# Layer norms of a two-layer decoder trunk: rows g and b applied to x later and on VectorE, their loads spread, a third weight block split ahead, and the order around the norm pinned

## The chip, the cores and the metric

One Trainium2 chip, one core of it. The metric is the device time of one execution in microseconds (us). A core has five engines that run side by side, each in the order of its own queue: TensorE (PE; matmuls and transposes), VectorE (DVE), ScalarE (ACT), GpSimd (POOL) and SyncE (SP, which here only issues DMAs). POOL issues DMAs too, through a queue of its own. They wait for each other by semaphores.

## The reference

A decoder trunk of two layers over 256 positions of width 2048, all in float32. Layer 0 mixes by a gated DeltaNet (GDN), layer 1 by sparse attention (DSA). What the change touches is the norm behind the mixer and behind the FFN, and what stands around it:

```python
def layer_norm(x, g, b):
    mu = mean(x); var = mean((x - mu) ** 2)
    return (x - mu) * rsqrt(var + LN_EPS) * g + b

for i in range(2):
    h = gdn_mixer(x, ...) if i == 0 else dsa_mixer(x, ...)
    x = layer_norm(DN_ALPHA * x + h, ln1_g[i], ln1_b[i])
    f = (silu(causal_dwconv(x @ ffn_w_gate[i])) * (x @ ffn_w_up[i])) @ ffn_w_down[i]
    x = layer_norm(DN_ALPHA * x + f, ln2_g[i], ln2_b[i])
    x = x + sigmoid(x @ ple_w_gate[i]) * (p[i] @ ple_w_proj[i])
```

## The kernel before

x lies in SBUF as two halves of 128 positions (a = 0, 1) by 2048. Every product with a weight matrix runs through `weights` (L89): a block of 128x1024 numbers (512 KB) is loaded by SP (`raw`, pool wp), rounded by ACT to the format that TensorE takes (`hi`), and DVE computes the rest, `lo` = raw − hi (both pool hl). TensorE then sums three products, x_hi·hi, x_lo·hi and x_hi·lo. The pools set how far this runs ahead: raw has 4 buffers, hi and lo have 2 each, so while TensorE works on one block the next is split, and further ones are being loaded. The splits carry a high priority (`W_AHEAD`), so the scheduler puts them early on ACT and DVE; the order on each engine is fixed when the program is built.

The two forms of product: in `gemm_t_steps` (GDN input, FFN gate and up) weights are stationary and the transposed activations move: x_hi and x_lo stand side by side as 512 columns (L117), then x_hi alone with lo as 256 (L121). In `gemm_steps` (the projections back to x, the PLE) the activations are stationary and 512 or 256 columns of weights move (L141, L142, L145).

`project` (the mixer's output or w_down) goes over five column blocks of x; behind each, DVE adds the residual (L214) and takes its statistics (L215). Behind the last one TensorE has two small products of the PLE (`fill`, L678 copies them to pw), meant for the time in which the norm's statistics are made. Then `layer_norm` (L241): DVE makes mean and 1/sqrt (a chain of twelve small instructions, L248 to L252), DVE and ACT normalise one half of x each, four pieces of 512 columns (L256, L257), TensorE transposes (L261, `n_ps`), ACT applies g and b, which lie along the partitions there, (L266, `xb`), and DVE splits the result into `xT` (L268 rounds, a CAST; L269 subtracts), the operand of the next products. The next product can begin with the first of eight xT pieces.

x itself gets g and b too, since it is added to the next residual: as rows along the columns. Rows of 512 columns (lng, lnb; broadcast to 128 partitions, 256 KB, two buffers each) are loaded by POOL (L194), and POOL multiplies and adds them (L274, L275): 16 instructions per norm, right behind it.

After the norm of the mixer comes the FFN: 20 pairs of column blocks, each gate and up (four weight blocks each), with the activation of gate ended by a Silu on ACT (L635). After the norm of the FFN comes the PLE: four column blocks of w_gate with 8 weight blocks each, the first two of them in turn. In layer 0's FFN, `distances` also writes the bias table `fx` for DSA to DRAM: four broadcasts of 766 KB (L724), issued by POOL as soon as fd is there.

GDN runs in eight groups. In each, SP carries a matrix L through DRAM and back (`lt` L464, `ld` L467), POOL makes inverses from it (L480, L482), which go back through `tt` and `pm` to TensorE (`w_ps`, L492). SP issues lt and ld in one queue with the loads of raw.

Of the kernel before, what the change touches and what calls it, by code (L numbers as in the profile page):

```python
# [63 lines left out]
class Trunk:  # L64
    def __init__(self, nc, tc, ctx, t):
# [21 lines left out]
        self.xT = self.xtp.tile([P, KT, 2, S], F32R, tag="xT", name="xT")  # L87


    def weights(self, src, rows, nk, cols):  # L90
# [8 lines left out]
        with self.tc.high_priority(offset=W_AHEAD):  # L99
            nc.scalar.activation(hi, raw, AF.Copy)  # L100
            nc.vector.tensor_tensor(lo, raw, hi.bitcast(F32), op=ALU.subtract)  # L101
# [27 lines left out]
    def gemm_steps(self, src, c0, n, x, kt, done):  # L129
# [5 lines left out]
        for k0 in range(0, kt, nk):  # L135
# [7 lines left out]
            for k in range(m):  # L143
                for a in range(2):
                    nc.tensor.matmul(ps[a][:, :n], x(k0 + k)[:, 0, a * P:(a + 1) * P], lo[:, k, :], start=False,  # L145
                                     stop=k0 + k == kt - 1)
# [44 lines left out]
    def rows(self, pool, src, n, tag, bufs=1):  # L191

        r = pool.tile([P, n], F32, tag=tag, name=tag, bufs=bufs)
        self.nc.gpsimd.dma_start(out=r, in_=bass.AP(tensor=src.tensor, offset=src.offset, ap=[[0, P], [1, n]]))  # L194
        return r
# [45 lines left out]
    def layer_norm(self, pool, st, g, b, gb):  # L241

        nc, x, xT = self.nc, self.x, self.xT
        with self.tc.high_priority():
# [7 lines left out]
            nc.vector.scalar_tensor_tensor(nm, mv[:, 1, 0:1], -1.0, r[:, 1:2], op0=ALU.mult, op1=ALU.mult)  # L252
            for k0 in range(0, KT, 2):
                if k0 % 4 == 0:
                    x0, x1 = (x[:, a, k0 * P:(k0 + 4) * P] for a in range(2))
                    nc.vector.tensor_scalar(x0, x0, mv[:, 0, 0:1], r[:, 0:1], op0=ALU.subtract, op1=ALU.mult)  # L256
                    nc.scalar.activation(x1, x1, AF.Identity, scale=r[:, 1:2], bias=nm)  # L257
                ps = self.sp.tile([P, 2, S], F32, tag="bk" if k0 % 4 else "sp", name="n_ps")
                for k in range(2):
                    for a in range(2):  # L260
                        nc.tensor.transpose(ps[:, k, a * P:(a + 1) * P], x[:, a, (k0 + k) * P:(k0 + k + 1) * P],  # L261
                                            self.ident)
                xb = pool.tile([P, 2, S], F32, tag="xb", name="xb", bufs=2)
                for k in range(2):
                    gk, bk = gb[:, k0 + k:k0 + k + 1], gb[:, KT + k0 + k:KT + k0 + k + 1]
                    nc.scalar.activation(xb[:, k], ps[:, k], AF.Identity, scale=gk, bias=bk)  # L266
# [3 lines left out]
        for nb in range(4):  # L270
            cs = slice(nb * 512, (nb + 1) * 512)
            gr, br = (self.rows(pool, r[cs], 512, k, 2) for r, k in ((g, "lng"), (b, "lnb")))
            for a in range(2):
                nc.gpsimd.tensor_tensor(x[:, a, cs], x[:, a, cs], gr, op=ALU.mult)  # L274
# [610 lines left out]
```

## Time and profile before

| | us |
|---|---|
| three runs | 2957.22, 2959.93, 2960.61 |
| median | 2959.93 |
| the profiled execution: its own time | 2958.56 |
| its span | 2956.8 |
| granted clock of TensorE, mean | 0.988 |
| loads of raw, 512 KB, issue to landing (median, most weights) | 3.6 |
| lng, lnb, 256 KB | 5.9, 6.2 |
| fx, 766 KB | 11.1 |
| POOL L274, one instruction (least, median, most) | 1.26, 1.51, 2.29 |
| DVE L268 CAST (least, median, most) | 0.41, 1.49, 1.52 |

The span goes from the first to the last instruction. A row of the timeline gives the start, the duration, the engine, the line and the operation, the tile written and those read, and in brackets how long the engine had been idle and what ended that. A row of windows gives, for a stretch from A to B, its length and the busy time of PE, of its weight loads, of DVE, ACT and POOL (with the number of instructions), then the granted clock, the busy share of the DMA engines and GB/s. A row of waits gives engine, tile and line, what it waited for, the sum, the number of times and the longest.

### The profile page before, as it was taken

To read this page: it belongs to the slowest core of one execution; us is meant where nothing else is said; L and a number is where in the kernel's file an instruction comes from. 1 tells how busy PE (TensorE), PEld (TensorE's weight loads), DVE (VectorE), ACT (ScalarE), POOL (GpSimd) and SP (SyncE) were. 2 spreads that over 40 slices of the span, in tenths; PEclk is the share of its full clock that TensorE was granted. 3 is DMA by queue.
4 is the path that set the end of the run, shared out by engine and by line. 5 is a ranking of instruction groups with operands and counts; after the bars stand their busy time and mean duration, and the time that the engine had idled before them with its cause. 6 is when DMAs were issued, how large, how long until landed. Compare 5 with 4: busy or idle time off the path is not lost. (4 is left out here: it accounts for less than half of the span.)

```text
span 2956.8 us, 41860 instructions
## 1 busy us (share of the span) xinstructions
PE 2842.5 (96%) x15790; PEld 2450.5 (83%) x15790; DVE 1904.7 (64%) x3080; ACT 1398.1 (47%) x2143; POOL 490.0 (17%) x780
## 2 busy tenths in 40 slices
PE   8899999999899899999999899999989999999989
PEld 6688888888679788888888788888878888888877
DVE  6678777788454856666554755656586666655475
ACT  4445455455333545555433444455355555543344
POOL 1543344543300300000000300120040000000030
PEclk9899999999999999999999999999999999999999
DMA  7555556655465566666555456554656666655545
GB/s 195 148 143 147 156 159 166 163 147 145 137 221 187 162 213 186 189 188 189 190 192 191 149 184 197 171 164 136 221 161 186 192 186 191 187 192 192 192 148 180
DMA packets 425883, 520.94 MB, mean 176 GB/s; under 512 B 28204, under 2 KB 329648, under 8 KB 425424
## 3 DMA queue, kind: packets, MB, share of 16 engines
q1 hardware_dynamic: 418576, 499.91, 55.8%
q0 software_dynamic: 7104, 18.35, 2.2%
q8 instruction: 124, 2.03, 0.3%
q14 instruction: 79, 0.65, 0.1%
HBM read 513.94 MB, written 7.39 MB: 176 GB/s over the span
## 5 line engine op out<-in xcount | busy, mean ns | idle before, releaser
L101 DVE TENSOR_TENSOR lo<-raw,hi 128x1024 fp32r<-128x1024 f32 x925 | 1161.5, 1257 | 883.5 <-ACT hi L100 863.3
L100 ACT ACTIVATE hi<-raw 128x1024 fp32r<-128x1024 f32 x925 | 977.3, 1057 | 1305.4 <-PE b_ps L142 563.8
L117 PE MATMUL mm_ps<-xT,hi 128*128 128x512 f32 x4176 | 1075.4, 397 | 13.2 <-ACT hi L100 7.9
L117 PEld LDWEIGHTS mm_ps<-xT,hi 128*128 128x128 f32 x4176 | 751.6, 190 | 149.0 <-ACT hi L100 9.0
L121 PEld LDWEIGHTS mm_ps<-xT,lo 128*128 128x128 f32 x4176 | 571.1, 190 | 46.9 <-DVE lo L101 7.8
L121 PE MATMUL mm_ps<-xT,lo 128*128 128x256 f32 x4176 | 594.8, 284 | 6.1 <-DVE lo L101 6.1
L274 POOL TENSOR_TENSOR x<-x,lng 128x512 f32<-128x512 f32 x32 | 51.4, 1626 | 1507.8 <-PE n_ps L261 1421.7
L141 PE MATMUL b_ps<-hi,xT 128*128 128x512 f32 (+2 forms) x736 | 276.1, 381 | 5.7 <-ACT hi L100 5.7
L142 PE MATMUL b_ps<-hi,xT 128*128 128x512 f32 (+2 forms) x736 | 276.5, 381 | 0.8 <-DVE xT L269 0.8
L141 PE MATMUL b_ps<-hi,hTA 128*128 128x512 f32 (+1 forms) x640 | 212.5, 347 | 0.0
L142 PE MATMUL b_ps<-hi,hTA 128*128 128x512 f32 (+1 forms) x640 | 212.3, 347 | 0.0
L145 PE MATMUL b_ps<-lo,xT 128*128 128x512 f32 (+2 forms) x736 | 196.5, 384 | 5.2 <-DVE lo L101 5.2
L141 PEld LDWEIGHTS b_ps<-hi,xT 128*128 128x128 f32 x736 | 139.6, 190 | 30.8 <-ACT hi L100 6.5
L142 PEld LDWEIGHTS b_ps<-hi,xT 128*128 128x128 f32 x736 | 140.0, 190 | 25.7 <-DVE xT L269 1.6
L145 PEld LDWEIGHTS b_ps<-lo,xT 128*128 128x128 f32 x736 | 133.0, 191 | 30.7 <-DVE lo L101 6.9
L145 PE MATMUL b_ps<-lo,hTA 128*128 128x512 f32 (+1 forms) x640 | 138.6, 347 | 0.0
L141 PEld LDWEIGHTS b_ps<-hi,hTA 128*128 128x128 f32 x640 | 121.2, 189 | 15.0
L142 PEld LDWEIGHTS b_ps<-hi,hTA 128*128 128x128 f32 x640 | 121.2, 189 | 15.0
L480 POOL TENSOR_TENSOR xt<-ld,xi 128x60 f32<-128x60 f32 (+24 forms) x248 | 116.7, 471 | 96.2 <-DMA ld<-lt 77.4
L145 PEld LDWEIGHTS b_ps<-lo,hTA 128*128 128x128 f32 x640 | 105.1, 189 | 15.0
L141 PE MATMUL b_ps<-hi,oT 128*128 128x512 f32 (+1 forms) x320 | 107.1, 350 | 3.4 <-ACT hi L100 3.4
L482 POOL TENSOR_TENSOR xi<-xi,xt 128x60 f32<-128x60 f32 (+24 forms) x248 | 106.9, 431 | 19.4
(260 smaller groups left out, 2727.2 us busy)
## 6 DMA issues: line engine op xcount, KB each, us to landing
raw<-in_gdn_w_in SPq DMA_DIRECT2D x193, 512.0 KB, 3.9
raw<-in_ffn_w_gate SPq DMA_DIRECT2D x160, 512.0 KB, 3.6
raw<-in_ffn_w_up SPq DMA_DIRECT2D x160, 512.0 KB, 3.6
raw<-in_ffn_w_down SPq DMA_DIRECT2D x160, 512.0 KB, 3.6
raw<-in_dsa_w_in SPq DMA_DIRECT2D x80, 512.0 KB, 3.6
raw<-in_gdn_w_o SPq DMA_DIRECT2D x64, 512.0 KB, 3.7
raw<-in_ple_w_gate SPq DMA_DIRECT2D x64, 512.0 KB, 4.2
raw<-in_dsa_w_o SPq DMA_DIRECT2D x32, 512.0 KB, 3.6
```

The lines of the kernel that those rows point to most:

```text
L100: nc.scalar.activation(hi, raw, AF.Copy)
L101: nc.vector.tensor_tensor(lo, raw, hi.bitcast(F32), op=ALU.subtract)
L117: nc.tensor.matmul(q[:m, :], hi[:, k, o:o + m], x[:, k0 + k].rearrange("p a b -> p (a b)"), start=k0 + k == 0, stop=False)
L121: nc.tensor.matmul(q[:m, S:], lo[:, k, o:o + m], x[:, k0 + k, 0, :], start=False, stop=k0 + k == kt - 1)
L141: nc.tensor.matmul(ps[a][:, :n], xh, hi[:, k, :], start=k0 + k == 0, stop=False)
L142: nc.tensor.matmul(ps[a][:, :n], xl, hi[:, k, :], start=False, stop=False)
L145: nc.tensor.matmul(ps[a][:, :n], x(k0 + k)[:, 0, a * P:(a + 1) * P], lo[:, k, :], start=False, stop=k0 + k == kt - 1)
L274: nc.gpsimd.tensor_tensor(x[:, a, cs], x[:, a, cs], gr, op=ALU.mult)
L480: nc.gpsimd.tensor_tensor(tmp[:, :m, :w], bcast(ld[:, i + 1:, i], m, 1), xi[:, :m, i:i + 1].to_broadcast([P, m, w]), op=ALU.mult)
L482: nc.gpsimd.tensor_tensor(xi[:, :m, i + 1:], xi[:, :m, i + 1:], tmp[:, :m, :w], op=ALU.subtract)
```

## The change

- hi and lo get three buffers each instead of two, raw three instead of four. To make room, GDN's `sq` shares a buffer with `y0`, and `ot` with `y` (two buffers).
- `layer_norm` takes over the order by explicit dependences: the splits of the next two blocks stand behind DVE's first piece of x (`behind`), the last copies of pw behind ACT's first piece, ACT's later pieces behind its xb, all transposes behind the last matmul of the fillers (`self.last`). The first piece of x is halved, to 256 columns.
- g and b on x: the 64 instructions move from POOL to DVE, out of the norm. For LN1 they are placed in the FFN, a quarter each after the steps n = 6, 14, 22, 30; the row loads wait for that step's last Silu (`self.mark`). For LN2 they are placed in the PLE behind the first three weight blocks of its first two column blocks, all four quarters, with no such wait. lng and lnb have one buffer each.
- fx is written in eight pieces of 383 KB, each behind the Silu of a step.

```diff
-        self.hl = pool(name="hl", bufs=2)
+        self.hl = pool(name="hl", bufs=3)
-        self.wp = pool(name="wp", bufs=4, side="right")
+        self.wp = pool(name="wp", bufs=3, side="right")
...
+    def after(self, ins, to, sync=False):
+        kind = mybir.DependencyClass.Sync if sync else mybir.DependencyClass.NoSync
+        self.tc.add_manual_dep(ins.ins, to.ins.name, mybir.DependencyInfo(kind, mybir.DependencyReason.DATA),
+                               reason="order")
...
-            nc.vector.tensor_tensor(lo, raw, hi.bitcast(F32), op=ALU.subtract)
+            ins = nc.vector.tensor_tensor(lo, raw, hi.bitcast(F32), op=ALU.subtract)
+        if self.behind:
+            self.after(ins, self.behind.pop())
...
-                if k0 % 4 == 0:
-                    x0, x1 = (x[:, a, k0 * P:(k0 + 4) * P] for a in range(2))
+                n = 2 if k0 < 4 else 0 if k0 % 4 else 4
+                if n:
+                    x0, x1 = (x[:, a, k0 * P:(k0 + n) * P] for a in range(2))
...
+                    if k0 >= 4:
+                        self.after(act, parts[k0 // 4 - 1])
+                    if not k0:
+                        self.behind = [dve] * 2
+                        for c in copies:
+                            self.after(c, act)
...
-        for nb in range(4):
-            gr, br = (self.rows(pool, r[cs], 512, k, 2) for r, k in ((g, "lng"), (b, "lnb")))
-            for a in range(2):
-                nc.gpsimd.tensor_tensor(x[:, a, cs], x[:, a, cs], gr, op=ALU.mult)
-                nc.gpsimd.tensor_tensor(x[:, a, cs], x[:, a, cs], br, op=ALU.add)
+        def affine(pool, nb, start):
+            gr, br = (self.rows(pool, r[cs], 512, k, 1, start) for r, k in ((g, "lng"), (b, "lnb")))
+            for a in range(2):
+                nc.vector.tensor_tensor(x[:, a, cs], x[:, a, cs], gr, op=ALU.mult)
+                nc.vector.tensor_tensor(x[:, a, cs], x[:, a, cs], br, op=ALU.add)
...
-                sq = pool.tile([P, 2, S], F32, tag="sq", name="sq")
+                sq = pool.tile([P, 2, S], F32, tag="y0", name="sq")
...
-                ot = pool.tile([P, 4, P], F32, tag="ot", name="ot")
+                ot = pool.tile([P, 4, P], F32, tag="y", name="ot", bufs=2)
...
+                if n in (6, 14, 22, 30):
+                    affine(pool, n // 8, self.mark)
...
+            for _ in range(3):
+                for g in steps[:2]:
+                    next(g)
+            for nb in range(4):
+                affine(pool, nb, None)
...
-        for o in range(0, R, R // 4):
+        for o in range(0, R, R // 8):
             yield
+            self.after(ins, self.mark, sync=True)
```

In the changed kernel's lines weights are L103 (raw), L107 (hi), L108 (lo); x is normalised on L270 and L271, transposed on L281, xb is L287, xT L290 and L291; rows of g and b are loaded on L203 and applied on L297 and L298.

The order on DVE at the first LN1, from the end of the statistics to the first xT pieces. Before:

```order
L238 SCALAR_TENSOR_TENSOR rs2_9302<-rt2_9303,rs2_9302 128x2
L101 TENSOR_TENSOR lo_9480<-raw_9477,hi_9479 128x1024
L252 SCALAR_TENSOR_TENSOR lnm_9316<-lmv_9297,rs2_9302 128x1
L256 TENSOR_SCALAR x_7845<-x_7845,lmv_9297,rs2_9302 128x512 x4
L268 CAST xT_84<-xb_9325 128x2x256
L269 TENSOR_TENSOR xT_84<-xb_9325,xT_84 128x2x256
```

After, at the same place:

```order
L249 SCALAR_TENSOR_TENSOR rs2_9302<-rt2_9303,rs2_9302 128x2
L264 SCALAR_TENSOR_TENSOR lnm_9316<-lmv_9297,rs2_9302 128x1
L270 TENSOR_SCALAR x_7845<-x_7845,lmv_9297,rs2_9302 128x256 x2
L270 TENSOR_SCALAR x_7845<-x_7845,lmv_9297,rs2_9302 128x512 x3
L108 TENSOR_TENSOR lo_9426<-raw_9423,hi_9425 128x1024
L108 TENSOR_TENSOR lo_9450<-raw_9447,hi_9449 128x1024
L290 CAST xT_84<-xb_9325 128x2x256
L108 TENSOR_TENSOR lo_9472<-raw_9469,hi_9471 128x1024
L291 TENSOR_TENSOR xT_84<-xb_9325,xT_84 128x2x256
```

Before, lo_9480 stands in the chain, and farther up, not shown, lo_9456 in the midst of the twelve small instructions and lo_9280 between the residual's statistics. After, the splits of the first FFN blocks stand between x and xT, three of them instead of two, and lo_9280 one residual earlier.

The order on DVE in the PLE of layer 0, from the end of the xT pieces on; lng and lnb are the rows of g and b. Before:

```order
L269 TENSOR_TENSOR xT_84<-xb_15532,xT_84 128x2x256
L101 TENSOR_TENSOR lo_15654<-raw_15651,hi_15653 128x1024
L101 TENSOR_TENSOR lo_15672<-raw_15669,hi_15671 128x1024
L101 TENSOR_TENSOR lo_15690<-raw_15687,hi_15689 128x1024
L101 TENSOR_TENSOR lo_15708<-raw_15705,hi_15707 128x1024
```

After:

```order
L298 TENSOR_TENSOR x_7845<-x_7845,lnb_15665 128x512
L108 TENSOR_TENSOR lo_15698<-raw_15695,hi_15697 128x1024
L297 TENSOR_TENSOR x_7845<-x_7845,lng_15671 128x512 x2
L108 TENSOR_TENSOR lo_15716<-raw_15713,hi_15715 128x1024
L298 TENSOR_TENSOR x_7845<-x_7845,lnb_15673 128x512 x2
L108 TENSOR_TENSOR lo_15734<-raw_15731,hi_15733 128x1024
L297 TENSOR_TENSOR x_7845<-x_7845,lng_15679 128x512 x2
L298 TENSOR_TENSOR x_7845<-x_7845,lnb_15681 128x512
L108 TENSOR_TENSOR lo_15752<-raw_15749,hi_15751 128x1024
L298 TENSOR_TENSOR x_7845<-x_7845,lnb_15681 128x512
```

Where splits followed each other, operations with rows stand between them now, and three more of these stand farther up between the xT pieces.

The order on SP in GDN, at group 7. Before:

```order
L96 DMA raw_7532<-in_gdn_w_in 128x2x512
L464 DMA lt_7055<-L_6974 32x8x32 x4
L96 DMA raw_7550<-in_gdn_w_in 128x2x512
L467 DMA ld_7060<-lt_7055 128x1x1024
L96 DMA raw_7568<-in_gdn_w_in 128x2x512
```

After:

```order
L103 DMA raw_7532<-in_gdn_w_in 128x2x512
L103 DMA raw_7550<-in_gdn_w_in 128x2x512
L489 DMA lt_7055<-L_6974 32x8x32 x4
L103 DMA raw_7568<-in_gdn_w_in 128x2x512
L492 DMA ld_7060<-lt_7055 128x1x1024
```

lt and ld each stand one load of raw later, in this group and in groups 1 to 6.

More of the change, by code (lines that the diff above doesn't have):

```diff
@@ L144, in gemm_steps @@
                 for a in range(2):
-                    nc.tensor.matmul(ps[a][:, :n], x(k0 + k)[:, 0, a * P:(a + 1) * P], lo[:, k, :], start=False,
-                                     stop=k0 + k == kt - 1)
+                    self.last = nc.tensor.matmul(ps[a][:, :n], x(k0 + k)[:, 0, a * P:(a + 1) * P], lo[:, k, :],
+                                                 start=False, stop=k0 + k == kt - 1)
             if k0 + m < kt:
@@ L189, in to_xT, with rows @@
         self.split(xT[:, k0:k0 + 4, 0, a * P:(a + 1) * P], xT[:, k0:k0 + 4, 1, a * P:(a + 1) * P], ps)
-    def rows(self, pool, src, n, tag, bufs=1):
+    def rows(self, pool, src, n, tag, bufs=1, start=None):
         r = pool.tile([P, n], F32, tag=tag, name=tag, bufs=bufs)
-        self.nc.gpsimd.dma_start(out=r, in_=bass.AP(tensor=src.tensor, offset=src.offset, ap=[[0, P], [1, n]]))
+        ins = self.nc.gpsimd.dma_start(out=r, in_=bass.AP(tensor=src.tensor, offset=src.offset, ap=[[0, P], [1, n]]))
+        if start is not None:
+            self.after(ins, start, sync=True)
         return r
@@ L239, in rsqrt, with layer_norm @@
         return y
-    def layer_norm(self, pool, st, g, b, gb):
+    def layer_norm(self, pool, st, g, b, gb, copies):
         nc, x, xT = self.nc, self.x, self.xT
@@ L260, in layer_norm @@
                     for a in range(2):
-                        nc.tensor.transpose(ps[:, k, a * P:(a + 1) * P], x[:, a, (k0 + k) * P:(k0 + k + 1) * P],
-                                            self.ident)
+                        ins = nc.tensor.transpose(ps[:, k, a * P:(a + 1) * P],
+                                                  x[:, a, (k0 + k) * P:(k0 + k + 1) * P], self.ident)
+                        self.after(ins, self.last)
                 xb = pool.tile([P, 2, S], F32, tag="xb", name="xb", bufs=2)
@@ L641, in up @@
                 self.split(hT(n)[:, 0], hT(n)[:, 1], h)
-            distances = self.distances(pool)
+            distances = self.distances(pool) if not i else iter(())
             for n in range(0, NF, 2):
```

49 lines of the change are left out of this document (27 added, 22 removed).

## The prediction

> **What bounds the kernel now.** I read the head of the page first, then the table of what TensorE waits for, then the windows around the waits.
>
> ```profile
> PE 2842.5 (96%) x15790; PEld 2450.5 (83%) x15790; DVE 1904.7 (64%) x3080; ACT 1398.1 (47%) x2143; POOL 490.0 (17%) x780
> ```
>
> TensorE (PE) is busy for 96% of the span, and no other engine is near that. So time is lost only where PE stands, and the change can gain no more than those places hold. The waits of PE, with the sum, the number and the longest of them:
>
> ```profile
> PE w_ps L492 <- DMA pm<-tt: 26.3, 2, 13.9
> ...
> PE b_ps L141 <- ACT hi L100: 9.0, 4, 2.8
> PE n_ps L261 <- DVE x L256: 8.8, 4, 2.2
> ...
> PE mm_ps L117 <- ACT hi L100: 7.9, 3, 3.5
> ...
> PE b_ps L145 <- DVE lo L101: 5.2, 4, 1.7
> ```
>
> Of these, those that come four times belong to the four layer norms. The windows show what they cost together: a quiet stretch first, then the first norm of a layer (LN1) and the second (LN2), both of layer 0.
>
> ```profile
> 900.00:950.00 50.00, 50.00 (x351) 47.04 (x350) 25.42 (x26) 19.06 (x18) 0.00 (x0) 1.00 0.60 188
> 963.00:1008.00 45.00, 35.56 (x190) 28.99 (x189) 42.87 (x54) 24.59 (x38) 29.39 (x20) 0.96 0.47 141
> 1661.00:1704.00 43.00, 33.56 (x143) 25.87 (x142) 40.21 (x49) 22.54 (x34) 28.75 (x20) 0.92 0.40 129
> ```
>
> In both, PE is idle for 9.4 us while VectorE (DVE, third busy time) is full: 42.87 of 45 us and 40.21 of 43. Inside a norm DVE is the bound. It is full for two reasons. The first is order, seen in its timeline (start, duration):
>
> ```profile
> 966.44 1.23 DVE L101 TENSOR_TENSOR lo<-raw,hi 128x1024 fp32r<-128x1024 f32 x1
> ...
> 969.45 1.23 DVE L101 TENSOR_TENSOR lo<-raw,hi 128x1024 fp32r<-128x1024 f32 x1
> ...
> 970.67 1.91 DVE L256 TENSOR_SCALAR x<-x,lmv,rs 128x512 f32<-128x512 f32 x4
> ```
>
> Splits of the blocks to come (lo) stand inside the chain of statistics, which ends where x is normalised (L256); a third one stands ahead of these two, as the rows of the order in the part on the change have it. The second reason is POOL:
>
> ```profile
> 972.51 2.67 POOL L274 TENSOR_TENSOR x<-x,lng 128x512 f32<-128x512 f32 x2 [152.93 <-PE n_ps L261]
> ...
> 984.51 0.58 POOL L194 DMA_DIRECT2D lng<-in_ln_g  x1
> ...
> 988.77 3.00 POOL L274 TENSOR_TENSOR x<-x,lng 128x512 f32<-128x512 f32 x2 [1.94 <-DMA lng<-in_ln_g]
> ```
> ```profile
> 975.65 1.51 DVE L268 CAST xT<-xb 128x512 fp32r<-128x512 f32 x1
> 977.20 1.64 DVE L269 TENSOR_TENSOR xT<-xb,xT 128x512 fp32r<-128x512 f32 x1
> ...
> 985.03 0.41 DVE L268 CAST xT<-xb 128x512 fp32r<-128x512 f32 x1
> 985.48 0.69 DVE L269 TENSOR_TENSOR xT<-xb,xT 128x512 fp32r<-128x512 f32 x1
> ```
>
> From 972.5 POOL multiplies and adds; beside it a piece of xT costs DVE 1.51 + 1.64 us. In POOL's pause (984.5 to 988.8, loads only) the same piece costs 0.41 + 0.69.
>
> **The change, term by term.** The profiled execution took 2958.56 us (span 2956.8 plus 1.8 around it), 1.4 under the median of the runs; the sum is made against 2958.56. Anything within 0.2% (some 6 us) a measurement of this kernel can't tell from no change.
>
> *LN1, twice.* PE's timeline of layer 0:
>
> ```profile
> 967.96 1.09 PE L145 MATMUL b_ps<-lo,pT 128*128 128x512 f32 x4
> 971.26 2.38 PE L261 MATMUL n_ps<-ident,x 128*128 128x128 f32 x17 [2.21 <-DVE x L256]
> ...
> 975.78 1.01 PE L117 MATMUL mm_ps<-xT,hi 128*128 128x512 f32 x3 [1.23 <-DVE xT L269]
> ...
> 1004.91 2.00 PE L117 MATMUL mm_ps<-xT,hi 128*128 128x512 f32 x8
> ...
> 1007.71 2.00 PE L117 MATMUL mm_ps<-xT,hi 128*128 128x512 f32 x8
> ```
>
> The last filler block ends near 969.1, the FFN's first matmul is at 975.78 and its ninth block at 1007.71; one undisturbed block is 2.8 (1007.71 − 1004.91). After: three lo's go out of the chain at 1.15 each (969.45 to just before 970.67), so x starts at 967.2. Its pieces on DVE (1.91 for four, now five with two of them halved) take some 2.2, two lo's 2.4, then CAST 0.41, lo 1.2, subtraction 0.69: the first matmul has its operand at 974.2, with handing over 974.5. PE has 24 transposes at 0.14 (2.38/17) ahead and 8 more behind (1.1), then eight blocks (22.4). Three are split already, and xT pieces come every 1.1 us instead of 3.15, so they run through (in the norm ACT's later x pieces, the pw copies and the transposes held behind the fillers only change places on engines that wait there anyway, so they cost nothing; if ACT lacked the time, rival 2 has the price): 974.5 + 1.1 + 22.4 = 998.0, with 0.4 for a late split 998.4. That is **−9.3 each, −18.6**. Bounds: −11.8 if nothing waits from 969.1 on (4.5 + 22.4 = 995.9), −3.4 if only the chain is shorter.
>
> *LN2, twice.*
>
> ```profile
> 1665.56 1.09 PE L145 MATMUL b_ps<-lo,pT 128*128 128x512 f32 x4
> ...
> 1702.86 1.07 PE L145 MATMUL b_ps<-lo,xT 128*128 128x512 f32 x4
> 1703.77 0.39 PE L141 MATMUL b_ps<-hi,xT 128*128 128x512 f32 x1
> ...
> 1705.58 1.07 PE L145 MATMUL b_ps<-lo,xT 128*128 128x512 f32 x4
> ```
>
> The fillers end at 1666.5 and the eighth PLE block starts at 1703.77; a block takes 2.72 (1705.58 − 1702.86). Without waits 32 transposes (4.5) and seven blocks (19.0) bring it to 1690.0. DVE needs the same run from lnm to the first xT piece, which costs PE about 0.9, and 0.9 for a late split: 1691.8, **−12.0 each, −24.0** (bounds −13.8 and −3.4).
>
> *Row operations on DVE.* The nearest row is
>
> ```profile
> L692 DVE TENSOR_TENSOR x<-x,sg x16: 678/686/694, 1728.6 to 2952.9; 128x512 f32<-128x512 f32 x16
> ```
>
> 64 of them at 0.69 are 44 us, spread over 16 quarters (2.7 each). In the FFN DVE is far from full (25.42 of 50 in the quiet window), so the work itself costs nothing. What can cost is the wait for the row: DVE works in order, so behind an x*g that waits for its load stand lo's for which PE waits. The load's time:
>
> ```profile
> DMA to landing us min/median/max: 3.5/5.9/9.5
> ```
> ```profile
> bias<-fx POOLq DMA_DIRECT2D x4, 256.0 KB, 4.7
> ```
>
> The 5.9 is for rows issued four at once; a row in its own comes nearer to 984.51 → 988.77 (4.3), and the 256 KB bias beside weight traffic took 4.7. I take 4.7. In the FFN the load leaves at the Silu, DVE does two lo's (one per 2.8 us), and comes to x*g 3 to 4 us later; it stands 1 to 2 us, while PE has blocks split for 4.5 us (POOL issues rows and fx pieces in turn, each behind the Silu of its own step, so none holds up the next): **0** (bounds 0 and +8, 1 us in each of eight). In PLE the order is tighter: row operations stand between the splits there, and each row has one buffer, so the load of lnb_15681 can leave only when DVE is done with lnb_15673. I followed it from 1661 with lo's of 1.2 and row operations of 0.69: the last use of lnb_15665 ends at some 1685.3; lnb_15673 lands at 1690.0 and its two operations end at 1691.4; lnb_15681 lands at 1696.1 and its operations, a lo between them, end at 1698.7; lnb_15689 lands at 1703.4, its operations end at 1704.8, and the lo behind them (the twelfth block's) at 1706.0. PE wants it at 1691.8 + 4 x 2.72 + 1.8 = 1704.5: **+1.5 each, +3**. With 4.3 a load it is 0.3, with 6.2 it is 6.0, since three loads stand in a row (bounds 0 and +12 for both layers). By the Trainium skill, DMA: Bandwidth & Descriptors, Anatomy of one DMA, a transfer of a POOL queue takes 2.0 us plus its bytes at 436 GB/s, an estimated 2.6 us for a row of 256 KB, and the term would be 0; the trace has nothing under 3.5, so I don't follow it.
>
> *fx.*
>
> ```profile
> 1071.94 1.11 PE L121 MATMUL mm_ps<-xT,lo 128*128 128x256 f32 x8
> 1076.54 3.78 PE L117 MATMUL mm_ps<-xT,hi 128*128 128x512 f32 x8 [3.48 <-ACT hi L100]
> ...
> 1083.94 1.11 PE L121 MATMUL mm_ps<-xT,lo 128*128 128x256 f32 x8
> ```
> ```profile
> fx<-fd POOLq DMA_DIRECT2D x4, 766.0 KB, 11.1
> ```
> ```profile
> 1076.50:1082.00 5.50, 5.46 (x17) 4.69 (x18) 2.45 (x2) 2.55 (x4) 0.00 (x0) 0.50 0.68 203
> ```
>
> Four pieces at once starve the weights. From one lo group to the one two blocks on are 12.0 us where two blocks are 5.6: 6.4 lost, 3.5 of them the wait and 2.9 the matmuls behind it, at a granted clock of 0.50. Pieces of half the size, one per two pairs of columns, should not do it: **−6.4** (other end 0).
>
> *Clock.* That row prices a pause of PE at up to its own length again. After the change each norm still has a pause of 1 to 2.5 us (PE waits for the first xT piece). Before, the transposes of LN2 behind a pause of 2.21 came at the lower clock, those of LN1 hardly. I add **+3** over four norms (bounds 0 and 4 × 2.9). The Trainium skill, TensorE: Matmul & The Clock Gate, Part 1, has half clock after an idle window of about 3.4 us that runs freely; by it the pauses left, all shorter, would mostly stay free and the term be near 0; the row behind 2.21 at LN2 (window's clock 0.92) speaks against that.
>
> *GDN.* Three blocks of raw weights instead of four, but three of hi/lo instead of two: six under way as before. Where the order of SP changes, lt and ld, which feed the inverses that w_ps waits for, each stand one raw later. In group 7 no other work covers that:
>
> ```profile
> 708.42 0.54 SPq L467 DMA_DIRECT2D ld<-lt  x1
> 712.25 0.39 SPq L96 DMA_DIRECT2D raw<-in_gdn_w_in  x1
> ```
>
> ld now stands behind raw_7568, which waits for a buffer and came at 712.25: ld at 712.6 instead of 708.42, and w_ps (the 26.3 above, of which this group is half) waits longer by as much. **+4** (bounds 0 and +4.2, as the splits may free the buffer sooner). In groups 1 to 6 other matmuls lie between; 0. The shared buffers of GDN (sq with y0, ot with y) make a square wait for the solve of the group before; the key blocks of the next group hide that, and without this cover eight groups would pay some 0.5 each: 0, bounds 0 and +4.
>
> Sum: −18.6 − 24.0 + 3 − 6.4 + 3 + 4 = −39.0; 2958.56 − 39.0 = **2919.6**.
>
> **Rivals.**
> 1. *Rows hold DVE.* Loads take 6.2 instead of 4.7 because weights run beside them. PLE then costs 6.0 each (9 more than in the sum), the FFN 1 us in each of eight: 2919.6 + 17 = 2937. For it: the median of 5.9; against: that median is of four at once. 0.15.
> 2. *ACT takes DVE's place in the norm.* Its rows:
>
> ```profile
> 970.78 1.52 ACT L257 ACTIVATE x<-x,lnm,rs 128x512 f32<-128x512 f32 x2 [0.59 <-DVE lnm L252]
> 972.24 1.93 ACT L266 ACTIVATE xb<-n_ps,gb 128x256 f32<-128x256 f32 x4
> ```
> Sixteen xb (0.48) are 7.7, x pieces 3.0, and hi's and pw copies stand between. If each hi comes behind and costs PE 3 us per norm: 2932. 0.10. The same number would come if the reordering left a lo in the chain (the change not doing what it says); the rows ordered after show none there.
> 3. *Slower.* One mechanism: an x*g that stands so long that PE runs dry, in all 16 quarters. In the FFN, DVE comes to x*g 3.3 us after the load's issue and may stand for 4.5: with a load of L us PE loses L − 7.8 in each of eight quarters. In PLE it loses 3 x (L − 4.2) in each layer. The 39 us are given back where 8 (L − 7.8) + 6 (L − 4.2) = 42, from L = 9.3 on; at L = 10 it is 2919.6 + 17.6 + 34.8 − 3 = 2969. For it: a row took up to 9.5 and the big fx pieces 11.1; against: both landed among other POOL loads. 0.06.
>
> **How the numbers follow.** Forecast 2919.6 with its own range 2908 to 2932: 0.64. Rivals 1 and 2, 2932 to 2945: 0.25, each with its own chance above. Within 0.2%: 0.05, slower 0.06. Low end: both norms at their better bounds (2 x 2.5 + 2 x 1.8 = 8.6) and the rows or the clock at 0 (3): 2908. High end: rival 1 with half of rival 2 on top: 2937 + 6.5 = 2944. Outside the range lie 0.03 below and 0.15 above: rival 3, no change, and 0.04 of the first two rivals. Faster: 0.64 + 0.25 = 0.89.
>
> **What would show it.** In the norm's windows POOL's busy time is gone and CAST takes 0.41 throughout; first FFN matmul about 1 us after before, ninth block 9 us. The waits of n_ps on x L256 vanish; that of hi at 1076 too. Wrong: PE waits on lo with DVE waiting on DMA lng or lnb; w_ps above 30 us.

## The result, and the profile after

Four runs of the changed kernel took 2910.35 to 2911.71 us, median 2911.0; four of the kernel before had a median of 2958.8. The ratio is 0.9838, with a 95% interval of 0.9821 to 0.9855: faster by 1.6%, 8.6 us below the predicted 2919.6 and inside its range. The profiled execution took 2910.35 us, its span is 2908.3.

The head of the page after, in the columns of the page before:

```profile
PE 2823.9 (97%) x15790; PEld 2444.7 (84%) x15790; DVE 1873.8 (64%) x3148; ACT 1394.7 (48%) x2147; POOL 399.7 (14%) x720
```

PE is busy for less time too (2842.5 before), with the same 15790 matmuls. At 1076 us, for one, they ran at half clock before, and do no longer. The waits of PE after:

```profile
PE w_ps L517 <- DMA pm<-tt: 31.3, 2, 16.4
...
PE n_ps L281 <- ACT xb L287: 6.5, 8, 1.5
...
PE g_ps L478 <- DVE ss L459: 4.1, 8, 1.4
PE b_ps L150 <- ACT sg L718: 2.4, 3, 1.1
...
PE b_ps L154 <- DVE lo L108: 1.7, 2, 1.1
```

In the norms the waits for x on DVE, for hi on ACT and for xT are gone, and those for lo are down to two. w_ps waits 5 us longer in its two places together. The windows, moved with the norms (LN1, LN2 of layer 0; the second begins some 2 us ahead of the work at which the one before began, in a stretch without a pause):

```profile
957.43:1002.43 45.00, 43.03 (x245) 36.67 (x245) 35.35 (x67) 31.58 (x50) 0.00 (x0) 1.00 0.52 164
1636.80:1679.80 43.00, 41.54 (x206) 34.28 (x206) 36.01 (x67) 25.55 (x38) 4.31 (x8) 1.00 0.61 190
```

PE's idle time in them fell from 9.4 us each to 2.0 and 1.5. DVE is no longer full (35.35 and 36.01 instead of 42.87 and 40.21), though it works for other blocks in the same windows. Its timeline at LN1:

```profile
961.93 0.16 DVE L264 SCALAR_TENSOR_TENSOR lnm<-lmv,rs 128x1 f32<-128x1 f32 x1
962.01 2.10 DVE L270 TENSOR_SCALAR x<-x,lmv,rs 128x256 f32<-128x256 f32 x5
964.03 2.35 DVE L108 TENSOR_TENSOR lo<-raw,hi 128x1024 fp32r<-128x1024 f32 x2
966.30 0.42 DVE L290 CAST xT<-xb 128x512 fp32r<-128x512 f32 x1
966.64 1.22 DVE L108 TENSOR_TENSOR lo<-raw,hi 128x1024 fp32r<-128x1024 f32 x1
967.77 0.68 DVE L291 TENSOR_TENSOR xT<-xb,xT 128x512 fp32r<-128x512 f32 x1
968.38 0.42 DVE L290 CAST xT<-xb 128x512 fp32r<-128x512 f32 x1
```

and the same stretch on PE:

```profile
963.49 1.25 PE L281 MATMUL n_ps<-ident,x 128*128 128x128 f32 x10
965.62 0.33 PE L281 MATMUL n_ps<-ident,x 128*128 128x128 f32 x1 [0.88 <-ACT xb L287]
966.53 0.33 PE L281 MATMUL n_ps<-ident,x 128*128 128x128 f32 x1 [0.58 <-ACT xb L287]
967.23 1.57 PE L281 MATMUL n_ps<-ident,x 128*128 128x128 f32 x12 [0.37 <-ACT x L271]
968.56 0.94 PE L126 MATMUL mm_ps<-xT,hi 128*128 128x512 f32 x3
...
972.71 2.00 PE L126 MATMUL mm_ps<-xT,hi 128*128 128x512 f32 x8
974.55 1.11 PE L130 MATMUL mm_ps<-xT,lo 128*128 128x256 f32 x8
975.50 2.00 PE L126 MATMUL mm_ps<-xT,hi 128*128 128x512 f32 x8
```

The transposes follow the fillers without a pause, every CAST takes 0.42 and from 968.56 on PE runs through. What is left are 1.8 us of pauses among the transposes, now behind ACT's xb and x. LN1 of layer 1 has the same pauses (0.87, 0.58, 0.37), but there PE ran at a lower clock from the fifth to the ninth us behind the last filler:

```profile
2129.43:2133.43 4.00, 4.00 (x16) 3.12 (x15) 3.33 (x7) 3.55 (x7) 0.00 (x0) 0.59 0.82 255
```

**Where the time went.** PE executes the same products in both kernels, so the start of the same matmul in the two traces, after minus before, gives the account place by place. All numbers of this kind below are made so, each from one execution of a kernel. Dense stretches in which nothing is changed agree to 0.02 us over hundreds of us. Other places vary without a change: up to group 7 of GDN, the six kernels below with the same order on every engine (after, on_pool, unpinned, rows_two, fx_four, pool_spread) lie 2.7 us apart, fx differs by 2.4 between kernels that issue it as before, and a norm by 1.0 to 1.5 with the clock.

| place | predicted | measured |
|---|---|---|
| start and GDN up to the wait of group 7 | 0 | −5.8 |
| w_ps of group 7 | +4 | +4.4 |
| first blocks of w_o | none | −4.0 |
| LN1, last filler to ninth FFN block (two layers) | −9.3, −9.3 | −10.0, −9.0 |
| clock in the norms | +3 | in the norms' rows |
| fx | −6.4 | −6.4 |
| rows in the FFN | 0 | 0.0 |
| LN2, last filler to eighth PLE block | −12.0, −12.0 | −12.4, −12.3 |
| rest of the PLE (rows) | +1.5, +1.5 | +3.0, +2.7 |
| start of DSA | none | +1.4 |
| sum, with 0.1 in other places | −39.0 | −48.5 |

### The profile page after: what moved, and what is told of

Same layout as the page of the kernel before. It is cut to its first block, busy times and chain, and to the rows that moved or that the text cites. A ratio compares the mean times of both kernels' runs of the same rounds, so it can differ in the third digit from the quotient of the medians.

```text
span 2908.3 us, 41890 instructions
## 1 busy us (share of the span) xinstructions
PE 2823.9 (97%) x15790; PEld 2444.7 (84%) x15790; DVE 1873.8 (64%) x3148; ACT 1394.7 (48%) x2147; POOL 399.7 (14%) x720
## 4 chain that ended last, share of the span: by engine, by line
PE 69%; issue 2%; DMA 2%; DVE 2%; ACT 1%; POOL 1%; DVEq 0%; SPq 0%; POOLq 0%; ACTq 0%
PE mm_ps L126 25%; PE mm_ps L130 13%; PE b_ps L154 10%; PE b_ps L150 9%; PE b_ps L151 9%; DMA lnb<-in_ln_b 1%; DVE lo L108 1%; ACT hi L107 1%; POOL xt L505 1%; PE s_ps L517 0%; POOL xi L507 0%; PE sc_ps L792 0%; DMA ld<-lt 0%; PE lg_ps L842 0%; DMA lng<-in_ln_g 0%
## 5 line engine op out<-in xcount | busy, mean ns | idle before, releaser
L108 DVE TENSOR_TENSOR lo<-raw,hi 128x1024 fp32r<-128x1024 f32 x925 | 1137.4, 1231 | 826.9 <-ACT hi L107 806.2
L107 ACT ACTIVATE hi<-raw 128x1024 fp32r<-128x1024 f32 x925 | 977.5, 1057 | 1279.3 <-PE b_ps L151 539.4
L126 PE MATMUL mm_ps<-xT,hi 128*128 128x512 f32 x4176 | 1062.0, 395 | 3.0 <-DVE rs L243 1.7
L203 POOL DMA_DIRECT2D lng<-in_ln_g x16 | 8.7, 546 | 1116.9 <-DVE lo L108 562.8
L150 PEld LDWEIGHTS b_ps<-hi,xT 128*128 128x128 f32 x736 | 138.9, 189 | 27.5 <-ACT sg L718 3.7
L507 POOL TENSOR_TENSOR xi<-xi,xt 128x60 f32<-128x60 f32 (+24 forms) x248 | 115.3, 465 | 19.4
```

What stands on the lines that cost most here:

```text
L108: ins = nc.vector.tensor_tensor(lo, raw, hi.bitcast(F32), op=ALU.subtract)
L126: nc.tensor.matmul(q[:m, :], hi[:, k, o:o + m], x[:, k0 + k].rearrange("p a b -> p (a b)"), start=k0 + k == 0, stop=False)
L150: nc.tensor.matmul(ps[a][:, :n], xh, hi[:, k, :], start=k0 + k == 0, stop=False)
L203: ins = self.nc.gpsimd.dma_start(out=r, in_=bass.AP(tensor=src.tensor, offset=src.offset, ap=[[0, P], [1, n]]))
L507: nc.gpsimd.tensor_tensor(xi[:, :m, i + 1:], xi[:, :m, i + 1:], tmp[:, :m, :w], op=ALU.subtract)
```

## The experiments

The changed kernel and its twelve variants, with the median of their runs and the ratio to the runs of the kernel before on the same chip, and by place as above (layer 0; us against before):

| kernel | median | ratio (95%) | GDN to group 7 | w_ps | w_o | LN1 | LN2 | PLE |
|---|---|---|---|---|---|---|---|---|
| after | 2911.0 | 0.9838 (0.9821–0.9855) | −5.8 | +4.4 | −4.0 | −10.0 | −12.4 | +3.0 |
| two_ahead | 2912.4 | 0.9855 (0.9840–0.9870) | −6.8 | +2.7 | −4.0 | −9.2 | −9.8 | +2.7 |
| on_pool | 2942.8 | 0.9955 (0.9940–0.9970) | −4.1 | +3.9 | −0.5 | +5.0 | −12.4 | +2.0 |
| unpinned | 2915.6 | 0.9862 (0.9847–0.9876) | −5.1 | +4.6 | −3.0 | −9.0 | −10.9 | +5.3 |
| rows_two | 2904.2 | 0.9822 (0.9805–0.9838) | −3.1 | +3.4 | −4.0 | −10.0 | −10.9 | 0.0 |
| ot_two | 2957.2 | 0.9998 (0.9989–1.0007) | −0.1 | −1.5 | −0.3 | +0.3 | −0.4 | 0.0 |
| rows_late | 2942.5 | 0.9946 (0.9931–0.9961) | +1.7 | −0.5 | −4.0 | −2.6 | −3.7 | 0.0 |
| dve_alone | 2911.8 | 0.9845 (0.9829–0.9862) | −5.8 | +1.8 | −4.0 | −9.2 | −11.1 | +2.6 |
| fx_four | 2910.7 | 0.9835 (0.9821–0.9850) | −4.2 | +1.8 | −3.2 | −8.8 | −10.9 | +2.7 |
| sq_y0 | 2953.1 | 0.9989 (0.9979–0.9998) | −4.5 | +1.6 | −0.4 | 0.0 | −0.4 | 0.0 |
| rows_two_ld | 2904.3 | 0.9821 (0.9806–0.9835) | −2.5 | +0.1 | −3.6 | −8.8 | −12.4 | 0.0 |
| two_rows_two | 2908.3 | 0.9837 (0.9822–0.9851) | −5.2 | +3.5 | −4.0 | −8.1 | −10.2 | 0.0 |
| pool_spread | 2914.1 | 0.9852 (0.9836–0.9869) | −4.4 | +3.3 | −4.0 | −10.0 | −9.9 | +4.0 |

**1. Without the third block (two_ahead).**

```diff
-        self.hl = pool(name="hl", bufs=3)
+        self.hl = pool(name="hl", bufs=2)
-        self.wp = pool(name="wp", bufs=3, side="right")
+        self.wp = pool(name="wp", bufs=4, side="right")
```

> The changed kernel with the pools of before: two buffers of hi and lo, four of raw. Stage T1 is from the end of the last filler to the start of the ninth FFN block at the first LN1 (38.7 us before, 28.8 after); T2 from there to the eighth PLE block at the first LN2 (37.3 before, 24.8 after). Theory A (the norms gain by order and by POOL being gone; the third block pays elsewhere): T1 30 to 31, T2 26 to 27, the two waits at the start of w_o (3.8 us) come back, the 0.7 us that each GDN group gained go, and w_ps of group 7 shortens by what GDN lost; together about 2922 us. Rival B (the third block is what carries the norms): T1 above 34, and 2935 us or more.

It took 2912.4. LN1 and LN2 gained nearly as much (T1 29.5, T2 27.5, the latter with a lower clock, 0.55 to 0.60 for 4 us), so the third block doesn't carry the norms; but the gains in GDN and at w_o, which theory A gave to it, stayed too. Their cause had to be looked for elsewhere.

**2. g and b on POOL behind LN1 (on_pool).**

```diff
+        self.norms = getattr(self, "norms", 0) + 1
+        if self.norms % 2:
+            for nb in range(4):
+                cs = slice(nb * 512, (nb + 1) * 512)
+                gr, br = (self.rows(pool, r[cs], 512, k, 2) for r, k in ((g, "lng"), (b, "lnb")))
+                for a in range(2):
+                    nc.gpsimd.tensor_tensor(x[:, a, cs], x[:, a, cs], gr, op=ALU.mult)
+                    nc.gpsimd.tensor_tensor(x[:, a, cs], x[:, a, cs], br, op=ALU.add)
+            return lambda *_: None
```

An odd count of norms is an LN1.

> The changed kernel, but g and b are applied on POOL behind LN1 of both layers, as before (LN2 keeps them on DVE). DVE's order at LN1 is that of after, row by row. Theory A (POOL's operations slow DVE beside them): CAST back to 1.5 us, T1 34 to 37, about 2911 + 2 x 7 = 2925 us. Rival (the order alone made the gain): CAST slow, but three blocks ahead cover it, T1 at most 30, 2911 to 2913 us.

It took 2942.8: 32 us more, over twice what theory A gave. With DVE's order as in the changed kernel, LN1 of layer 0 took 5.0 us more than before the change and lost another 2.9 in the FFN behind it (layer 1: 3.8 and 1.7); of w_o's gain of 4.0, 0.5 was left. POOL and DVE in this stretch of it:

```profile
980.58 2.57 POOL L299 TENSOR_TENSOR x<-x,lng 128x512 f32<-128x512 f32 x2
983.09 2.52 POOL L300 TENSOR_TENSOR x<-x,lnb 128x512 f32<-128x512 f32 x2
985.58 2.47 POOL L299 TENSOR_TENSOR x<-x,lng 128x512 f32<-128x512 f32 x2
988.02 2.47 POOL L300 TENSOR_TENSOR x<-x,lnb 128x512 f32<-128x512 f32 x2
```
```profile
976.66 1.66 DVE L291 TENSOR_TENSOR xT<-xb,xT 128x512 fp32r<-128x512 f32 x1
...
979.79 0.69 DVE L291 TENSOR_TENSOR xT<-xb,xT 128x512 fp32r<-128x512 f32 x1
980.40 10.38 DVE L290 CAST xT<-xb 128x512 fp32r<-128x512 f32 x1
```

Besides the slow pieces known from before (1.66) there is one CAST of 10.38 us, just as long as POOL had eight operations in a row, each at its full speed of 1.25. The order alone gains nothing while POOL runs in the norm.

**3. Without the explicit order (unpinned).**

```diff
     def after(self, ins, to, sync=False):
+        if not sync:
+            return
```

> The changed kernel without the explicit order of the norm (no lo behind x, no copies behind ACT's x, no transposes behind the fillers, no x pieces behind xb; the waits of the row loads for the Silu stay). Three lo's stand inside the chain of statistics again. Theory A: x starts 3.4 us later, of which the three blocks ahead win back what then no longer stands between x and xT (2 lo's): T1 30 to 32, about 2911 + 4 x 2 = 2919 us. Rival (with POOL gone order no longer matters): T1 at most 29.3, 2911 to 2913 us.

It took 2915.6. By place, and with the same clock in either trace, the pins are worth 1.0 and 0.2 us at the LN1s and 1.5 and 1.2 at the LN2s; the PLE lost 2.3 more in layer 0 and 0.9 less in layer 1. That is theory A's direction, at half its size. The total doesn't show it clearly: the intervals of the two ratios overlap, and dve_alone (7.), also without the pins, took 2911.8.

**4. Two buffers for the rows in the PLE (rows_two).** The timelines of DVE and POOL of the changed kernel show what was to be tested:

```profile
1662.37 0.54 POOL L203 DMA_DIRECT2D lnb<-in_ln_b  x1 [7.91 <-DVE x L298]
...
1669.45 0.54 POOL L203 DMA_DIRECT2D lnb<-in_ln_b  x1 [4.20 <-DMA lng<-in_ln_g]
...
1676.50 0.54 POOL L203 DMA_DIRECT2D lnb<-in_ln_b  x1 [4.18 <-DVE x L298]
```
```profile
1667.86 1.29 DVE L298 TENSOR_TENSOR x<-x,lnb 128x512 f32<-128x512 f32 x2 [2.20 <-DMA lnb<-in_ln_b]
...
1673.77 0.69 DVE L298 TENSOR_TENSOR x<-x,lnb 128x512 f32<-128x512 f32 x1 [2.28 <-DMA lnb<-in_ln_b]
...
1680.91 1.29 DVE L298 TENSOR_TENSOR x<-x,lnb 128x512 f32<-128x512 f32 x2 [1.38 <-DMA lnb<-in_ln_b]
1682.12 3.49 DVE L108 TENSOR_TENSOR lo<-raw,hi 128x1024 fp32r<-128x1024 f32 x3
```
```profile
1683.40 1.20 PE L154 MATMUL b_ps<-lo,xT 128*128 128x512 f32 x4 [1.06 <-DVE lo L108]
1696.55 0.50 PE L150 MATMUL b_ps<-hi,xT 128*128 128x512 f32 x1 [1.05 <-ACT sg L718]
```

Each load leaves when DVE is done with the row before, DVE stands until it lands, three lo's come in a heap behind, and PE waits.

```diff
-            gr, br = (self.rows(pool, r[cs], 512, k, 1, start) for r, k in ((g, "lng"), (b, "lnb")))
+            gr, br = (self.rows(pool, r[cs], 512, k, 1 if start is not None else 2, start) for r, k in ((g, "lng"), (b, "lnb")))
```

> The changed kernel with two buffers each of lng and lnb in the PLE. Theory A (each row's load waits for DVE to be done with the row before it, DVE waits for the load, PE for the lo behind): the 3.0 and 2.6 us that PE loses between the eighth PLE block and the end of the PLE go, about 2905.5 us. Rival (what PE loses there comes from ACT's sigmoid and the late raws of three blocks ahead): at least 1 us of it stays in each PLE, 2908 us or more.

It took 2904.2, the best median here: the loss of 3.0 and 2.7 is 0.0 in both PLEs, the pause for ACT's sigmoid at 1696.55 included, which was a consequence of the heap. Theory A holds.

**5. Only ot's second buffer, on the kernel before (ot_two).**

```diff
-                ot = pool.tile([P, 4, P], F32, tag="ot", name="ot")
+                ot = pool.tile([P, 4, P], F32, tag="y", name="ot", bufs=2)
```

> The kernel before, with one edit: ot of GDN takes the two buffers of y instead of its one. Theory C (the 0.6 to 0.8 us that each GDN group gained come from ot's second buffer, since two_ahead kept them without the third block): 4 to 6 us less by the end of group 6's matmuls, of which the wait for the inverses of group 7 takes back all but 1 to 2; the total 2954 to 2957 against 2957 before. Rival (they come from the changed order around the norm or from sq): nothing, under 1 us before group 7.

No difference, and −0.1 before group 7. Theory C fell.

**6. Only the row loads later, on the kernel before (rows_late).**

```diff
+        if start is not None:
+            self.tc.add_manual_dep(ins.ins, start.ins.name, mybir.DependencyInfo(
+                mybir.DependencyClass.Sync, mybir.DependencyReason.DATA), reason="order")
...
-            gr, br = (self.rows(pool, r[cs], 512, k, 2) for r, k in ((g, "lng"), (b, "lnb")))
+            gr, br = (self.rows(pool, r[cs], 512, k, 2, self.last if nb < 2 else None) for r, k in ((g, "lng"), (b, "lnb")))
```

Here `self.last` is the last matmul of the fillers, as in the changed kernel.

> The kernel before, with one edit: POOL's loads of the first two quarters of g and b wait for the last filler matmul, instead of leaving as soon as their buffers are there (LN1 of layer 0: at 805 us, in the first blocks of w_o). Theory D (these four loads of 256 KB starve the weights, which is what PE lost at the start of w_o: 3.8 us gone in every kernel that doesn't load them there, and kept in on_pool, which does): 3.8 to 4 us less between 796 and 846 us; the norms within 1 us of before, so about 2953. Rival (the wait there is the switch from GDN to w_o and its splits): under 0.5 us.

2942.5: the 4.0 us at w_o are there, as theory D has it. The total lies 10 us under its 2953, because the norms gained too, by 1.9 to 3.7 each. In layer 0 POOL's first operation comes 2.1 us later behind the last filler at LN1 and 1.6 later at LN2, and the first xT piece of LN1 takes 0.43 + 0.69. That the later start makes the whole of this gain is not shown: the clock differs between the traces as well.

**7. Of the norm's part only the move to DVE (dve_alone).** The edits of two_ahead and unpinned together, and the first piece of x undivided; the spread of fx and the shared buffers of sq and ot stay:

```diff
-                n = 2 if k0 < 4 else 0 if k0 % 4 else 4
+                n = 0 if k0 % 4 else 4
```

> The changed kernel with two buffers of hi and lo, four of raw, no explicit order of the norm and an undivided first piece of x: of the norm's part only the move to DVE with its spread loads stays (and fx, sq, ot). Theory E (POOL's operations beside DVE are most of it): LN1 (last filler to ninth FFN block) 7 to 8 us less than before, LN2 8 to 9 less, about 2915 to 2920 us. Rival (the parts only work together): LN1 and LN2 less than 5 us shorter than before, 2925 or more.

2911.8, the same as the whole change. LN1 gained 9.2 and 8.9, LN2 11.1 and 10.7, each 1 to 2 us more than theory E gave. Theory E holds: taking the row operations out of the norm is most of the gain there.

**8. fx in four pieces (fx_four).**

```diff
-        for o in range(0, R, R // 8):
+        for o in range(0, R, R // 4):
```

> The changed kernel with fx in four pieces of 766 KB, as before, each behind the Silu of a step. Theory F (what starved the weights was that four pieces ran at once, 3 MB; one alone is covered by the blocks ahead): no wait of PE in the FFN, the 6.4 us stay gained. Rival (a piece must be small): PE waits 0.5 us or more at each of the four, 2 to 8 us back.

2910.7, the 6.4 us stay gained, and PE waits at none of the four. It is the spreading, not the size.

**9. Only sq's shared buffer, on the kernel before (sq_y0).**

```diff
-                sq = pool.tile([P, 2, S], F32, tag="sq", name="sq")
+                sq = pool.tile([P, 2, S], F32, tag="y0", name="sq")
```

> The kernel before, with one edit: sq of GDN shares y0's buffer. Its squares then wait for the solve of the group before, and lt and ld of group 7 stand one raw later on SP, as in the changed kernel. Theory G (ot alone gave nothing, so this sharing is where the 0.6 to 0.8 us per group come from, by moving the squares and sums to another place in PE's order): 4 to 6 us less before group 7, 2 to 4.4 us of it taken back by w_ps; 2954 to 2956 against 2957. Rival (only both shared buffers together, or something outside GDN): under 1 us before group 7, and w_ps longer by what ld comes later.

2953.1, with −4.5 before group 7 and +1.6 at w_ps. Theory G holds: a buffer shared to save room changed the order of the work in GDN, 826 of PE's matmuls stand at another place, and the gain came with that. Which of the moves makes it was not separated. The trace has another −2.1 at fx, where nothing was changed.

**10. lt and ld ahead again (rows_two_ld).** rows_two, and this:

```diff
         raw = self.wp.tile(shape, F32, tag="raw", name="raw")
-        nc.sync.dma_start(out=raw, ...)
+        ins = nc.sync.dma_start(out=raw, ...)
+        if self.queue:
+            to = self.queue.pop(0)
+            if to is not None:
+                self.after(ins, to)
...
         def zgate(s):
+            if s["g"] == 7:
+                self.queue = [None, s["lt"], s["ld"]]
```

`s["lt"]` and `s["ld"]` are the issues of lt and ld of the group.

> rows_two (2904.2 us), and in group 7 SP has lt ahead of the second and ld ahead of the third raw of the gate's projection, as before the change. Theory H (ld stands behind a raw that waits for a buffer): ld leaves 2 us or more earlier relative to lt's issue, w_ps gives 2 to 4 us back, 2900 to 2902. Rival (the wait of group 7 grew because PE comes 5.8 us earlier to inverses that POOL makes no sooner; ld's place costs little): under 1 us, 2903 to 2905.

SP at group 7, with the pins and without (rows_two):

```profile
704.16 1.81 SPq L494 DMA_DIRECT2D lt<-L  x4
706.07 0.40 SPq L104 DMA_DIRECT2D raw<-in_gdn_w_in  x1
707.33 0.53 SPq L497 DMA_DIRECT2D ld<-lt  x1
```
```profile
704.94 1.94 SPq L489 DMA_DIRECT2D lt<-L  x4
709.46 0.39 SPq L103 DMA_DIRECT2D raw<-in_gdn_w_in  x1
710.03 0.53 SPq L492 DMA_DIRECT2D ld<-lt  x1
```

ld follows lt by 3.2 us instead of 5.1 (the other traces have 3.2 with the old order of SP and 5.1 with the new), and w_ps costs +0.1 against before instead of +3.4. By place that is theory H; the total is 2904.3, no less than rows_two's 2904.2. PE's gain up to and behind w_ps is 2.4 us here, and fx_four, dve_alone and sq_y0 have 2.4 to 4.0 with ld in the later place: what POOL does between ld and tt took 44.2 to 47.0 us in the fourteen traces, and that differs by more than the 1.9 us of ld's place. So that ld leaves earlier is shown, and that it makes the kernel faster is not.

**11. rows_two without the third block (two_rows_two).**

The edits of rows_two and two_ahead together.

> rows_two with two buffers of hi and lo and four of raw. Theory I (the third block buys back only what waiting for rows costs, and what it wins at the norms it loses at the starts of PLE and DSA): within 3 us of rows_two's 2904.2, either way. Rival (without the stalls for rows the third block shows its 2.6 us per LN2 and 0.8 per LN1): 2909 or more.

2908.3, some 4 us above rows_two, between the two theories and clear of neither; the intervals of the two ratios overlap. LN1 gained 8.1 and 8.5 us instead of 10.0 and 10.2, but at the lower clock in both layers, which alone costs 1.0 to 1.2 (fx_four). The FFNs lost 1.1 and 2.2, and they lost 0.5 to 1.0 in the two other kernels with two blocks and 0.0 in those with three (on_pool apart). So the third block has a place where it pays; in the total its few us are not clear.

**12. The same places, but POOL (pool_spread).**

```diff
-                nc.vector.tensor_tensor(x[:, a, cs], x[:, a, cs], gr, op=ALU.mult)
-                nc.vector.tensor_tensor(x[:, a, cs], x[:, a, cs], br, op=ALU.add)
+                nc.gpsimd.tensor_tensor(x[:, a, cs], x[:, a, cs], gr, op=ALU.mult)
+                nc.gpsimd.tensor_tensor(x[:, a, cs], x[:, a, cs], br, op=ALU.add)
```

> The changed kernel with the 64 operations on x back on POOL, at the same places (LN1's in the FFN behind a Silu, LN2's in the PLE). Theory J (what hurt was POOL's work inside the norm, where DVE is full, not POOL as such; in the FFN DVE has half its time free): LN1 as in the changed kernel, 9 to 10 us under before; nothing lost in the FFN; LN2, whose operations still begin among the xT pieces, 5 to 12 us longer; 2915 to 2935 us. Rival K (wherever POOL runs beside DVE, a lo or a CAST stands for as long as POOL has work in a row, as in on_pool, and PE runs dry): PE loses 2 us or more in each of the eight FFN quarters too, 2935 or more.

2914.1. LN1 as in the changed kernel, 0.0 lost in the FFN, although DVE runs slowly beside POOL there as well:

```profile
1063.22 2.28 DVE L664 TENSOR_TENSOR fh<-fh,fac 128x256 f32<-128x256 f32 x2
1065.42 2.31 DVE L108 TENSOR_TENSOR lo<-raw,hi 128x1024 fp32r<-128x1024 f32 x1
```

Theory J holds, and its price for LN2 was too high (2.1 to 2.5 us against the changed kernel, not 5 to 12). Part of that is the clock: both LN2s ran at 0.50 for some 2 us, as LN2 of layer 0 in rows_two did, which lost 1.5 by it. With one buffer a row, the loads hold POOL's operations apart, so only some of the xT pieces meet one. Not the engine but the place made most of the gain.

## Why the prediction was right, and where its steps failed

- **LN1 and LN2** came as summed (−42.6 against −43.7). But the sum gave 3.4 us of each norm to the order and the rest to POOL, with the third block beside them. By dve_alone, POOL's leaving the norm has −9.2 of −10.0 at LN1 and −11.1 of −12.4 at LN2, and by unpinned the order adds 0.2 to 1.5. The three lo's that left the chain stand between x and the first xT piece now (2.35 + 1.22 us in the timeline), so most of what the chain lost comes back behind it.
- **fx** came to a tenth of a us, clock included, and that is partly luck. ot_two and sq_y0 issue fx as before and lose 4.2 and 4.3 us there, behind pauses of 2.41 and 2.53 us instead of 3.48; rows_late loses 6.6. The step said that half the size would do it; fx_four shows that one at a time does.
- **Rows in the FFN**: 0, as said. **Rows in the PLE**: the mechanism was right (rows_two), its size was 3.0 and 2.7 instead of 1.5. A row took 4.3 to 5.5 us from issue to use (1662.37 to 1667.86, 1669.45 to 1673.77) where 4.7 was taken, and the heap of lo's had a second pause in its train. The 2.6 us that the prediction estimated from the Trainium skill, DMA: Bandwidth & Descriptors, is not seen: the least of lng is 3.6, of lnb 4.1.
- **w_ps**: +4.4 where +4 was said, but not by the step as it was given. The step had ld at 712.6 instead of 708.42. After the change it left at 707.65:

```profile
702.56 1.94 SPq L489 DMA_DIRECT2D lt<-L  x4
...
707.65 0.53 SPq L492 DMA_DIRECT2D ld<-lt  x1
```

lt left 2.7 us earlier than before, as GDN was ahead; behind lt, ld came 1.9 later. w_ps starts at 761.92 instead of 763.73, and PE, which had gained 5.8, waits for the difference. So a good part of +4.4 is GDN's own gain, which the sum had at nothing, and the agreement is in part luck. Other kernels with the same order of SP paid 1.6 to 4.6.
- **GDN otherwise**: priced at 0 with bounds of 0 and +4, it was −5.8. The step took a shared buffer for a risk only. It is also a change of order, which sq_y0 alone shows as −4.5. The five other kernels with the same order have −3.1 to −5.1, and two with the order of before −0.1 and +1.7, so some of the 5.8 is chance.
- **The first blocks of w_o**: the step that failed is the reading of "b_ps L141 <- ACT hi: 9.0, 4" as four norms. Two of the four were in w_o, while row loads of POOL were under way, eight of 256 KB that left from 805 to 819:

```profile
805.01 0.60 POOL L194 DMA_DIRECT2D lng<-in_ln_g  x1
...
813.23 0.56 POOL L194 DMA_DIRECT2D lng<-in_ln_g  x1
```
```profile
815.84 0.50 PE L141 MATMUL b_ps<-hi,oT 128*128 128x512 f32 x1 [1.29 <-ACT hi L100]
...
820.94 0.50 PE L141 MATMUL b_ps<-hi,oT 128*128 128x512 f32 x1 [2.08 <-ACT hi L100]
```

The changed kernel issues them in the FFN and the PLE. rows_late shows the 4.0 us by themselves. A look at where each of the four stood would have given them.
- **Clock**: +3 was added over four norms; in the profiled execution one of the four had it, LN1 of layer 1 (−9.0, at the clock of 0.59 shown above, where LN1s of the same order at full clock had −10.0 and −10.2), so the term was 1.0 to 1.2. It comes without a difference in the kernel: with the same pauses (0.88, 0.58, 0.37) rows_two_ld ran LN1 of layer 0 at a lower clock for 4 us and lost 1.2 us against the changed kernel. Windows from the fifth to the ninth us behind the last filler, of rows_two_ld and of after:

```profile
967.96:971.96 4.00, 4.00 (x17) 3.24 (x16) 3.33 (x7) 3.55 (x7) 0.00 (x0) 0.62 0.76 245
```
```profile
968.49:972.49 4.00, 3.86 (x26) 2.98 (x25) 3.33 (x7) 3.92 (x8) 0.00 (x0) 1.00 0.77 252
```

So the term is 0 or 1.0 to 1.2 for an LN1, by chance; for an LN2 it was 1.5 (rows_two, layer 0: −10.9). That it comes and goes fits the freely running window of the Trainium skill, TensorE: Matmul & The Clock Gate, Part 1; that pauses of under 1 us bring it does not fit its 3.4 us of idleness.
- **DSA's start**: +1.4, not foreseen. It is 0.6 or less in the variants of the changed kernel with two blocks ahead (two_ahead, dve_alone, two_rows_two) and in unpinned, but ot_two, with two blocks as before, has +2.2. As ot_two changes nothing there, it may be no effect of the change at all. In the trace after, PE waits 1.65 us at 1772 for rs on DVE, where it waited 0.34 before. No run was made for its cause, and it stays open.

Of the 9.5 us between sum and trace, GDN has 5.8, w_o 4.0, the clock 3.0 and the norms 1.1 on one side, PLE and DSA 4.1 and w_ps 0.4 on the other; that the forecast landed within 0.3% owes something to these two sides. Rival 1's mechanism was there in the PLE, at 5.7 us for both layers where it gave 12, and not in the FFN; rival 2's waits for hi and rival 3 were not seen, though the 1.8 us of pauses left in a norm are behind ACT. Both signs named for being wrong appeared, PE waiting on lo behind the loads of lnb and w_ps above 30 us (31.3), and neither made the change fail; the mark of 30 for w_ps lay below what the sum itself gave (26.3 + 4).

## What to carry to other kernels

An auxiliary engine that works beside the critical one is best moved out of the stage in which that one is full, even without changing the engine: the place gave the gain. Large loads that don't matter yet should leave one at a time, behind an event of the stage that has room for them; loads issued as early as their buffers allow cost 4 and 4.2 to 6.6 us here in stages that had nothing to do with them. A buffer shared to save room can change the order of a whole stage, for better or worse, so look at the order after it. Where a wait stands in a table four times, look where each of the four is before giving them to one cause.

## What the runs showed of the hardware

- A CAST on DVE that takes 0.42 us alone, and some 1.5 beside POOL in the kernel before, stood for 10.38 us while POOL ran eight operations of 1.25 back to back. The Trainium skill, SBUF — State Buffer, SBUF: two separate sides, says that the two engines share a pair of ports that one holds for a whole instruction while the other waits; here DVE did not get it between POOL's instructions either. Why it took turns in other stretches (1.5 each) stays open.
- Behind a pause of 3.48 us PE ran at a granted clock of 0.50 for some 5 us, so that the pause cost 6.4. Behind pauses of 2.41 and 2.53 us (ot_two, sq_y0) the clock was 0.54 and 0.55 for 3.6 us. Behind three short pauses among transposes it was 0.59 for 4 us in one norm of the changed kernel and 1.00 in the three others.
